# Two-level block product b of the output projection: earlier loads of w_out, its sums and y's on different engines, another order of splits

## The chip, the cores and the metric

The kernel runs on one core of a Trainium2 chip. The metric is the device time of one execution in microseconds, from the first to the last instruction of the core with what the launch adds around it. The kernel before took 803.74 us, the median of three runs (803.44 to 803.85).

## What is computed

One layer of a short-convolution mixer with a sandwich norm, on 1024 tokens of width 1024, with an inner width of 2048, all in float32:

```python
def short_conv_mixer(u, w_in, conv_w, w_out):
    z, bg, cg, v = jnp.split(u @ w_in.astype(u.dtype), 4, axis=-1)
    y = bg * causal_dwconv(cg * v, conv_w) * jax.nn.silu(z)
    return y @ w_out.astype(u.dtype)

# DEPTH is 1, so the layer is
u = rms_norm(x, pre_norm[0])
out = x + rms_norm(short_conv_mixer(u, sc_w_in[0], sc_conv_w[0], sc_w_out[0]), post_norm[0])
```

`u @ w_in` is 1024x1024 by 1024x8192, `y @ w_out` is 1024x2048 by 2048x1024.

## The kernel before

**Products.** Every matrix product is done as a 2x2 block product with seven block products instead of eight, called a, b, c, e, d, f, g. Products c, d, e, f and g take sums or differences of blocks as operands, a and b take plain blocks. Each operand is split into a high part (ScalarE rounds it to fp32r, L154) and a low part (VectorE subtracts the high part from the operand, L155), and each product is three matmuls: low times high, high times low, high times high.

**First stage.** The 2048 inner channels are 16 chunks of 128 columns. A chunk is two pairs: the even pair holds the columns of cg and v, the odd one those of z and bg; END = 31 is the last pair. From chunk 3 on the two pairs' products b are done together with a second level of the same scheme, seven small products a' to g' with 256 moving columns. The list `slots` is the order in which TensorE takes the products: for pair 31 it is a(31), e', g(30), c(31), f', e(31), d', d(31), f(31), g', g(31). After every slot the loop at L852 emits by hand what the other engines do then: weights' sums on GpSimd (`add_s`), splits (`prepare`), the convolution (L578 on ScalarE, L581 on VectorE), gates. Every engine works off its own instructions strictly in this written order. The finished chunk of y (`cv`) goes to DRAM (`y_d`, L243); `add_y` (L254) forms the sums of y that the last stage's products need and stores them in `s_d`; `add_t` does the same for w_out in `t_d`.

**Last stage.** y is the stationary side and w_out the moving side. Every block product but b is two halves h of four pages of 128x512; a half is `out_mm` on four PSUM banks, 48 matmuls of 512 columns. A half's operands come from `load_unit` (four loads of 256 KB each on SP's queue), and `split_unit` splits them into a buffer of the pool `up`, which has seven such buffers for both stages. Pages come from one pool of 36; a load or a sum that takes a page waits until the page's last reader is done.

**Product b of the last stage** has a second level of its own, `product_b` (L1052): seven small products `small_mm` of 24 matmuls with 256 columns, in the order a', b', e', c', d', f', g'. Its operands:

- `bu[0]`, `bu[1]`: the two groups of four pages of w_out; `by[0]`, `by[1]`: the same for y.
- `out_t` (L745) makes w_out's sums, four GpSimd instructions of 128x256 for each of four k: L754 changes the second half of `bu[0]` in place, L755 and L756 fill the pages `bu["cd"]`, L758 fills `bu["x"]`.
- `out_s` (L760) makes y's sums: kind "d" (L765) changes the second half of `by[0]` in place, kind "s" (L774 to L776) fills `by["ec"]` and `by["x"]`, which need `by[1]`.
- `out_split` splits them: A1 is `by[0]` after "d", A2 is `by[1]`, A3 is `by["ec"]`; B1 is `bu[0]` after L754, B2 is `bu[1]` as loaded, B3 is `bu["cd"]`; X is both "x". a' reads A1 and B1, b' reads A2 and B2, e' A3 and B1, c' A3 and B3, d' A1 and B3, f' X and B2, g' A2 and X. In the profile these are the tiles oA_b, oB_b and ox_b, the loaded pages ru_b and ry_b, the sums t_b and s_b, and the small products' banks pb_x, pb_y, pb_v.
- after each small product `small_add` (VectorE, L1050) adds its bank to `acc`. a', c', d' and g' share the bank pb_x, so c' must wait for the add of a', d' for that of c', g' for that of d'. Between these adds VectorE's order holds other splits: after the add of b' the four of X, after that of e' the four of the next unit (ou_c), and only then the add of c'.

`combine("a", q)` (L1003, ScalarE) copies the result of product a from PSUM to `acc`; `acc` lies where `cv` lay, so these copies also wait for the last `add_y`. B3's rounding stands behind them on ScalarE.

Of the kernel before, what the change touches and what calls it, by code (L numbers as in the profile page):

```python
# [21 lines left out]
def kernel(  # L22
# [16 lines left out]
    nc = tc.nc  # L39
# [5 lines left out]
    NC = CI // P  # L45
# [25 lines left out]
    def page(name, dtype=F32, shape=(HB,)):  # L71

        return pages.tile([P, *shape], dtype, tag="pg", name=name, bufs=PAGES)
# [79 lines left out]
    def split(src, hi, lo):  # L153
        nc.scalar.copy(hi, src)  # L154
        nc.vector.tensor_sub(lo, src, hi.bitcast(F32))  # L155
# [98 lines left out]
    def add_y(c):  # L254

        if c < CH:
            cv = done.pop(c)
            t = page(f"s3_{c}")
            nc.vector.tensor_sub(t, cv[:, :HB], cv[:, HB:])
            nc.sync.dma_start(s_d[:, SK["d"], c], t)  # L260
        else:
            cv, (t0, t1) = done.pop(c), far_y.pop(c)
            t2 = page(f"s4_{c}")
            nc.vector.tensor_add(t1, t1, cv[:, HB:])
            nc.vector.tensor_sub(t0, t1, t0)
            nc.vector.tensor_sub(t2, cv[:, :HB], t0)
            for k, t in zip("cef", (t0, t1, t2)):
                nc.sync.dma_start(s_d[:, SK[k], c - CH], t)
# [435 lines left out]
    CQ = CH // 2  # L704
    fetched, OP = [], {}

    def load_unit(side, i, h):
        js = slice(h * CQ, (h + 1) * CQ)
        far = slice(CH + h * CQ, CH + (h + 1) * CQ)
        if side == "u":  # L710
            plain_u = {"a": wov[:, js, :HB], "b": wov[:, far, :HB], "f": wov[:, far, HB:]}
            src = plain_u[i] if i in plain_u else t_d[:, TK[i], js]
        else:
            plain_y = {"a": y_d[:, js, :HB], "b": y_d[:, far, :HB], "g": y_d[:, far, HB:]}
            src = plain_y[i] if i in plain_y else s_d[:, SK[i], js]
        r = [page(f"r{side}_{i}{h}{k}") for k in range(CQ)]
        for k in range(CQ):
            nc.sync.dma_start(r[k], src[:, k])
        return r

    def fetch_unit():
        n = len(fetched)
        if n < len(UNITS):
            fetched.append(load_unit(*UNITS[n]))
# [8 lines left out]
    def split_pages(src, name):  # L733
        t = up.tile([P, 2, CQ, HB], F32R, tag="u", name=f"o{name}")
        for k in range(CQ):
            split(src[k], t[:, 0, k], t[:, 1, k])
        return t
# [4 lines left out]
    bu, by = {}, {}  # L742
    FB, SB = slice(0, HH), slice(HH, HB)

    def out_t(ks):  # L745

        for k in ks:
            b0, b1 = bu[0][k], bu[1][k]
            if k == 0:
                bu["cd"] = []  # L750
                bu["x"] = [page(f"t4_b{j}") for j in range(CQ // 2)]
            t = page(f"t23_b{k}")
            bu["cd"].append(t)
            nc.gpsimd.tensor_sub(b0[:, SB], b0[:, SB], b0[:, FB])  # L754
            nc.gpsimd.tensor_sub(t[:, FB], b1[:, SB], b0[:, SB])  # L755
            nc.gpsimd.tensor_sub(t[:, SB], t[:, FB], b0[:, FB])  # L756
            x = bu["x"][k // 2][:, k % 2 * HH : (k % 2 + 1) * HH]
            nc.gpsimd.tensor_sub(x, b1[:, FB], t[:, FB])  # L758

    def out_s(ks, kinds):  # L760

        for k in ks:
            a0, a1 = by[0][k], by[1][k]
            if kinds == "d":
                nc.gpsimd.tensor_sub(a0[:, SB], a0[:, FB], a0[:, SB])  # L765
                continue
            if k == 0:
                by["ec"] = []
                by["x"] = [page(f"s4_b{j}") for j in range(CQ // 2)]
            t = page(f"s12_b{k}")  # L770
            by["ec"].append(t)
            x = by["x"][k // 2][:, k % 2 * HH : (k % 2 + 1) * HH]

            nc.gpsimd.tensor_sub(t[:, SB], a1[:, SB], a0[:, SB])  # L774
            nc.gpsimd.tensor_add(t[:, FB], t[:, SB], a0[:, FB])
            nc.gpsimd.tensor_sub(x, a1[:, FB], t[:, SB])  # L776


    OUT_A = {"a'": ("A1", 0), "d'": ("A1", HH), "b'": ("A2", 0), "g'": ("A2", HH), "e'": ("A3", 0), "c'": ("A3", HH)}
# [3 lines left out]
    def out_split(n):  # L783
        if n == "X":
            t = up.tile([P, 2, 2, CQ, HH], F32R, tag="u", name="ox_b")
            for z, src in enumerate((by["x"], bu["x"])):
                for j in range(CQ // 2):
                    split(flat2(src[j]), t[:, z, 0, 2 * j : 2 * j + 2], t[:, z, 1, 2 * j : 2 * j + 2])
            ob_w[n] = t
        else:  # L790
            src = {"A1": (by, 0), "A2": (by, 1), "A3": (by, "ec"), "B1": (bu, 0), "B2": (bu, 1), "B3": (bu, "cd")}[n]
            ob_w[n] = split_pages(src[0][src[1]], f"{n}_b")

    def flat2(t):
        return t.rearrange("p (a b) -> p a b", b=HH)

    END = len(PAIRS) - 1
    TODO = {p: j for j, p in enumerate([8, 10, 12, 13, 14, 15, 16, 17])}

    def odd_t(p, steps):  # L800
        if p % 2 and p in TODO:
            add_t(TODO[p], steps)
# [32 lines left out]
    at, t = [], 0.0  # L835
# [16 lines left out]
    for n, (i, p) in enumerate(slots):  # L852
        if i[1:]:
            deep_product(p, i)
            prepare(n)
            deep_after(p, i)
            if i == "f'":
                odd_t(2 * p + 1, [0, 1])
            elif i == "g'":
                nc.scalar.activation(sn[2 * p + 1, "a"], sn[2 * p + 1, "a"], AF.Silu)  # L860
                odd_t(2 * p + 1, [3])
            continue
        product(p, i)
        prepare(n)
        after(p, i)
        q, prev = p + 1, p // 2 - 1
        if p == 2:
            first_chunk(i)
        if i == "c":
            if p % 2 and p // 2 < DEEP:  # L870
                nc.scalar.activation(sn[p, "a"], sn[p, "a"], AF.Silu)
            if p % 2 == 0 and p in TODO:
                fetch_t(TODO[p])
            if p % 2 == 0 and p > 2:
                fetch_s(prev)
            if p % 2 == 0 and p // 2 >= DEEP:
                deep_sums(p // 2, 1)
        elif i == "e":
            add_s(q, "ec")
        elif i == "d":  # L880
            if p + 2 <= END:
                fetch(p + 2)
            add_s(q, "d")
            if p in TODO and p % 2 == 0:
                add_t(TODO[p])
            if p % 2 == 0 and p > 2:
                add_y(prev)
        elif i == "f":
            add_s(q, "f")
            if p == 2:  # L890
                add_y(0)
        elif i == "g":
            if p % 2 and q <= END and q // 2 >= DEEP:
                deep_sums(q // 2, 0)
        elif i == "a":
            if p % 2 and p in TODO:
                fetch_t(TODO[p])
        if DEEP < NC and (i, p) in UNDER:
            UNDER[i, p]()
        if p == END - 1 and i in "cd":  # L900
            fetch_unit()
        if p == END:
            if i in "acdg":
                split_unit()
            if i in "ac":
                fetch_unit()
            if i in "ce":
                bu["ce".index(i)] = load_unit("u", "b", "ce".index(i))
            if i == "d":
                by[0] = load_unit("y", "b", 0)  # L910
                out_t([0, 1])
            elif i == "f":
                fetch_s(NC - 1)
                out_t([2, 3])
            elif i == "g":
                by[1] = load_unit("y", "b", 1)
                out_s(range(CQ), "d")
                out_s(range(CQ), "s")
    mixed.close()
    p2 = ctx.enter_context(tc.tile_pool(name="p2", bufs=1, reuse_waits="tile"))  # L920

# [96 lines left out]
    def finish_row(t):  # L1018
        finish(t)
        if t + 2 < NT:  # L1020
            load_res(t + 2)
# [40 lines left out]
                for q in (0, 1) if i == "f'" else (2, 3):  # L1062
                    early_half(q)

    for i in ("A1", "B1"):
        out_split(i)
    add_y(NC - 1)
    out_split("A2")
    for n, (i, h) in enumerate(OUT[:-2]):
        if i == "b":  # L1070
            if h == 0:
                product_b()
            continue
        if (i, h) == ("f", 0):
            load_res(0)
            load_res(1)
        for q in range(TH):
            out_mm(i, h, q)
        if i == "a":
            if h == 0:  # L1080
                out_split("B2")
                out_split("A3")
                fetch_unit()
        else:
            for _ in "uy":
                split_unit()
                fetch_unit()
        if h == 1:
            for q in range(TH):
                combine(i, q)  # L1090
                if i == "f" and q > 0:
                    finish_row(q - 1)
            if i == "a":
                out_split("B3")
# [31 lines left out]
```

## Time and profile before

| | |
|---|---|
| time, median of 3 runs | 803.74 us (803.44 to 803.85) |
| the profiled execution: its time | 806.15 us |
| its span, first to last instruction | 804.3 us |
| TensorE busy | 783.3 us, 97% of the span |
| VectorE busy | 620.2 us, 77% |
| GpSimd busy | 393.8 us, 49% |
| ScalarE busy | 341.2 us, 42% |
| mean granted TensorE clock | 0.99 |

How to read it: times of an engine's rows count from the span's start. A busy TensorE is not one at its peak, since matmuls are pipelined and overlap in the records; the distance between starts tells the rate. "idle before <- releaser" names what the engine had last waited for. Lines of the kernel are written L155; a helper's line stands for all its uses, so groups are told apart by the tiles that they write and read.

### The profile page before, as it was taken

How to read it: one execution, taken by the hardware profiler on the slowest of the kernel's cores; microseconds unless marked ns; L12 is line 12 of the kernel's file. 1: busy time of each engine (PE TensorE's matmuls, PEld its weight loads, DVE VectorE, ACT ScalarE, POOL GpSimd, SP SyncE). 2: the span in 40 equal slices, each digit the busy share in tenths (PEclk: the TensorE clock that was granted, in tenths of full speed). 3: DMA queues.
4: the chain of work that ended last, by engine and by line, in shares of the span. 5: the costliest groups of instructions: out<-in, count | busy, mean ns of one | idle time of the engine just before them, and what ended most of it. 6: DMA issues, size and time to landing. Idle time of an engine off the chain costs nothing.

```text
span 804.3 us, 11017 instructions
## 1 busy us (share of the span) xinstructions
PE 783.3 (97%) x3800; PEld 661.3 (82%) x3800; DVE 620.2 (77%) x847; ACT 341.2 (42%) x622; POOL 393.8 (49%) x289
## 2 busy tenths in 40 slices
PE   9999999999999999999999999999999968999995
PEld 8888888888888888888888888888888858888884
DVE  6899667978777888888686867768688698844665
ACT  7555425343424342434433343434345174655431
POOL 2616579646647373748483746556471970000020
PEclk9999999999999999999999999999999988999999
DMA  9111330407162565654150606152339469753047
GB/s 335 34 53 37 109 117 28 138 21 236 47 202 84 203 187 199 199 177 157 53 172 26 196 2 195 39 158 78 119 106 318 159 220 376 254 187 108 1 126 241
DMA packets 108329, 114.53 MB, mean 142 GB/s; under 512 B 6585, under 2 KB 72177, under 8 KB 108273
## 3 DMA queue, kind: packets, MB, share of 16 engines
q1 hardware_dynamic: 108256, 113.82, 43.1%
q8 instruction: 30, 0.49, 0.3%
q14 instruction: 27, 0.21, 0.1%
q10 hardware_dynamic: 16, 0.00, 0.0%
HBM read 84.44 MB, written 29.36 MB: 141 GB/s over the span
## 4 chain that ended last, share of the span: by engine, by line
PE 87%; DMA 4%; DVE 3%; POOL 2%; ACT 1%; issue 1%; POOLq 0%; DVEq 0%; SPq 0%; ACTq 0%
PE px L189 14%; PE px L188 14%; PE px L190 14%; PE pv L188 7%; PE pv L189 7%; PE pv L190 7%; DMA xr<-in_x 2%; PE po_x L946 2%; PE po_x L948 2%; PE po_x L947 2%; PE po_v L948 2%; PE po_v L946 2%; PE po_v L947 2%; PE px L687 1%; PE px L686 1%; PE px L685 1%
## 5 line engine op out<-in xcount | busy, mean ns | idle before, releaser
L217 POOL TENSOR_TENSOR sne<-sne,cv 128x512 f32<-128x512 f32 x15 | 25.1, 1672 | 161.4 <-DVE sne L215 161.4
L988 POOL TENSOR_TENSOR acc<-acc,xr 128x512 f32<-128x512 f32 x4 | 6.5, 1624 | 121.1 <-DVE acc L987 117.9
L581 DVE SCALAR_TENSOR_TENSOR cv<-gpad,cw,cv 128x1024 f32<-128x1024 f32 x32 | 42.0, 1313 | 17.3 <-ACT cv L578 16.7
L155 DVE TENSOR_TENSOR wel<-se,weh 128x512 fp32r<-128x512 f32 x31 | 52.1, 1682 | 3.2 <-ACT weh L154 3.2
L146 POOL TENSOR_TENSOR se<-raw,raw 128x512 f32<-128x512 f32 x31 | 52.2, 1684 | 3.0 <-PE px L190 2.5
L150 POOL TENSOR_TENSOR sf<-raw,sc 128x512 f32<-128x512 f32 x31 | 53.0, 1710 | 0.0
L148 POOL TENSOR_TENSOR sc<-se,raw 128x512 f32<-128x512 f32 x31 | 50.1, 1617 | 2.4
L196 ACT COPY snc<-px 128x512 f32<-128x512 f32 x31 | 18.2, 586 | 73.3 <-PE px L190 73.3
L225 POOL TENSOR_TENSOR gpad<-snc,sne 128x512 f32<-128x512 f32 x15 | 20.1, 1339 | 59.3 <-DVE snc L220 59.3
L188 PE MATMUL pv<-u_e,wel 128*128 128x512 f32 x124 | 48.6, 392 | 0.0
L188 PE MATMUL px<-u_g,wgl 128*128 128x512 f32 x124 | 48.5, 391 | 0.0
L189 PE MATMUL px<-u_d,wdh 128*128 128x512 f32 x124 | 48.6, 392 | 0.0
L189 PE MATMUL pv<-u_e,weh 128*128 128x512 f32 x124 | 48.6, 392 | 0.0
L189 PE MATMUL px<-u_a,wah 128*128 128x512 f32 x124 | 48.6, 392 | 0.0
L188 PE MATMUL px<-u_a,wal 128*128 128x512 f32 x124 | 48.6, 392 | 0.0
L196 ACT COPY sna<-px 128x512 f32<-128x512 f32 x30 | 17.5, 583 | 73.2 <-PE px L190 48.7
L188 PE MATMUL px<-u_d,wdl 128*128 128x512 f32 x124 | 48.5, 391 | 0.0
L189 PE MATMUL px<-u_g,wgh 128*128 128x512 f32 x124 | 48.4, 391 | 0.0
L188 PE MATMUL pv<-u_f,wfl 128*128 128x512 f32 x124 | 48.3, 390 | 0.0
L188 PE MATMUL px<-u_c,wcl 128*128 128x512 f32 x124 | 48.2, 389 | 0.0
L190 PE MATMUL px<-u_a,wah 128*128 128x512 f32 x124 | 48.2, 389 | 0.0
L190 PE MATMUL px<-u_c,wch 128*128 128x512 f32 x124 | 48.2, 389 | 0.0
(409 smaller groups left out, 2610.2 us busy)
## 6 DMA issues: line engine op xcount, KB each, us to landing
raw<-in_sc_w_in SPq DMA_DIRECT2D x128, 256.0 KB, 4.2
y_d<-cv SPq DMA_DIRECT2D x16, 512.0 KB, 3.0
s_d<-s SPq DMA_DIRECT2D x32, 256.0 KB, 2.3
t<-in_sc_w_out SPq DMA_DIRECT2D x32, 256.0 KB, 4.2
t_d<-t SPq DMA_DIRECT2D x32, 256.0 KB, 2.6
s<-y_d SPq DMA_DIRECT2D x16, 256.0 KB, 4.2
xr<-in_x SPq DMA_DIRECT2D x16, 256.0 KB, 4.9
xa<-in_x SPq DMA_DIRECT2D x4, 512.0 KB, 5.1
```

Source lines behind the costliest of these rows:

```text
L146: nc.gpsimd.tensor_add(t, block(p, 1, 0), block(p, 1, 1))
L148: nc.gpsimd.tensor_sub(t, sums[p, "e"], block(p, 0, 0))
L150: nc.gpsimd.tensor_sub(t, block(p, 0, 1), sums[p, "c"])
L155: nc.vector.tensor_sub(lo, src, hi.bitcast(F32))
L188: nc.tensor.matmul(ps, lo, UH[i][:, k], start=first and k == 0, stop=False, skip_group_check=True)
L189: nc.tensor.matmul(ps, hi, UL[i][:, k], start=False, stop=False, skip_group_check=True)
L190: nc.tensor.matmul(ps, hi, UH[i][:, k], start=False, stop=last, skip_group_check=True)
L196: nc.scalar.copy(t, banks[p, "v" if i == "e" else "x"])
L581: nc.vector.scalar_tensor_tensor(cv, gpad[:, j : j + L], tap(c, j), cv, op0=ALU.mult, op1=ALU.add)
L946: nc.tensor.matmul(ps, lo, u[:, 0, k], start=first, stop=False, skip_group_check=True)
L947: nc.tensor.matmul(ps, hi, u[:, 1, k], start=False, stop=False, skip_group_check=True)
L948: nc.tensor.matmul(ps, hi, u[:, 0, k], start=False, stop=last, skip_group_check=True)
```

## The change

Three things move, and no computation is added or left out:

- y's sums for product b, `out_s`, go from GpSimd to VectorE, four instructions of kind "d" and twelve of kind "s".
- The eight loads of w_out's blocks (`bu`) move from slots c and e of pair 31 to slots d and f of pair 30, and so ahead of the second units' loads of product a on SP's queue; w_out's sums (`out_t`) move from d and f of pair 31 to c and e of pair 31. On GpSimd they now stand ahead of the last pair's gates (L217, L223) instead of around them.
- The order of splits. Before: A1, B1, `add_y`, A2, then B2 and A3. After, in VectorE's order: B2, B1, the four "d", A1, the twelve "s", A2, A3, `add_y`, with B3 behind as before.

```diff
@@ out_s @@
             if kinds == "d":
-                nc.gpsimd.tensor_sub(a0[:, SB], a0[:, FB], a0[:, SB])
+                nc.vector.tensor_sub(a0[:, SB], a0[:, FB], a0[:, SB])
                 continue
...
-            nc.gpsimd.tensor_sub(t[:, SB], a1[:, SB], a0[:, SB])
-            nc.gpsimd.tensor_add(t[:, FB], t[:, SB], a0[:, FB])
-            nc.gpsimd.tensor_sub(x, a1[:, FB], t[:, SB])
+            nc.vector.tensor_sub(t[:, SB], a1[:, SB], a0[:, SB])
+            nc.vector.tensor_add(t[:, FB], t[:, SB], a0[:, FB])
+            nc.vector.tensor_sub(x, a1[:, FB], t[:, SB])
@@ the loop over slots @@
+        if p == END - 1 and i in "df":
+            bu["df".index(i)] = load_unit("u", "b", "df".index(i))
         if p == END:
             if i in "acdg":
                 split_unit()
             if i in "ac":
                 fetch_unit()
             if i in "ce":
-                bu["ce".index(i)] = load_unit("u", "b", "ce".index(i))
+                out_t(([0, 1], [2, 3])["ce".index(i)])
             if i == "d":
                 by[0] = load_unit("y", "b", 0)
-                out_t([0, 1])
             elif i == "f":
                 fetch_s(NC - 1)
-                out_t([2, 3])
             elif i == "g":
                 by[1] = load_unit("y", "b", 1)
+                out_split("B2")
+                out_split("B1")
                 out_s(range(CQ), "d")
-                out_s(range(CQ), "s")
+                out_split("A1")
@@ ahead of the last stage's products @@
-    for i in ("A1", "B1"):
-        out_split(i)
-    add_y(NC - 1)
-    out_split("A2")
@@ after product a's first half @@
             if h == 0:
-                out_split("B2")
+                out_s(range(CQ), "s")
+                out_split("A2")
                 out_split("A3")
+                add_y(NC - 1)
                 fetch_unit()
```

## The prediction

> **What bounds the kernel now.** The page first: TensorE is busy for nearly the whole span.
>
> ```profile
> span 804.3 us, 11017 instructions
> PE 783.3 (97%) x3800; PEld 661.3 (82%) x3800; DVE 620.2 (77%) x847; ACT 341.2 (42%) x622; POOL 393.8 (49%) x289
> ```
>
> So only what TensorE waits for, or does slowly, can be won. Its waits over the whole span, longest first:
>
> ```profile
> PE pb_x L1043 <- DVE acc L1050: 3.6, 1, 3.6
> PE pb_y L1044 <- DVE oB_b L155: 2.8, 1, 2.8
> PE pb_y L1043 <- DVE oA_b L155: 2.7, 1, 2.7
> ```
>
> All three lie in product b of the last stage, and all end on VectorE. Busy time by stretch (after the stretch: its length, then PE, PEld, DVE, ACT, POOL; the granted clock is behind the engines):
>
> ```profile
> 660.00:670.00 10.00, 8.53 (x57) 8.35 (x58) 9.90 (x18) 6.44 (x14) 0.00 (x0) 0.77 1.02 355
> 670.00:680.00 10.00, 6.38 (x37) 6.18 (x36) 7.83 (x14) 3.18 (x6) 0.00 (x0) 0.74 1.05 400
> 700.00:710.00 10.00, 10.00 (x46) 8.29 (x45) 1.27 (x3) 3.08 (x7) 0.00 (x0) 1.00 0.37 129
> 780.00:790.00 10.00, 10.00 (x46) 8.29 (x45) 7.87 (x21) 1.61 (x6) 3.03 (x2) 1.00 0.84 254
> ```
>
> Product b also runs at a lower clock (0.77, 0.74), while from 700 on TensorE is full at clock 1.00: a gain in product b reaches the end whole. TensorE's order of time there:
>
> ```profile
> 627.44 0.39 PE L946 MATMUL po_x<-ou_a,oy_a 128*128 128x512 f32 x1
> 649.20 0.28 PE L1043 MATMUL pb_x<-oB_b,oA_b 128*128 128x256 f32 x1
> 658.07 0.55 PE L1043 MATMUL pb_y<-oB_b,oA_b 128*128 128x256 f32 x1 [2.72 <-DVE oA_b L155]
> 675.48 0.58 PE L1043 MATMUL pb_x<-oB_b,oA_b 128*128 128x256 f32 x1 [3.62 <-DVE acc L1050]
> 675.86 0.41 PE L1044 MATMUL pb_x<-oB_b,oA_b 128*128 128x256 f32 x1
> 676.08 0.41 PE L1045 MATMUL pb_x<-oB_b,oA_b 128*128 128x256 f32 x1
> 686.81 0.28 PE L1045 MATMUL pb_x<-ox_b,oA_b 128*128 128x256 f32 x1
> 686.93 0.40 PE L946 MATMUL po_x<-ou_c,oy_c 128*128 128x512 f32 x1
> ```
>
> Product b takes 37.7 us (649.20 to 686.93). Its 168 matmuls at the late spacing of 0.12 (686.81 to 686.93) would need 20.2. After a gap they start 0.21 apart (675.86 to 676.08). The start at 675.48 is d', which waited for VectorE's add of c'.
>
> VectorE's order of time up to that add:
>
> ```profile
> 630.92 0.72 DVE L230 TENSOR_TENSOR cv<-cv,sna 128x512 f32<-128x512 f32 x1 [0.29 <-ACT sna L860]
> 631.56 5.21 DVE L155 TENSOR_TENSOR oy_a<-ry_a,oy_a 128x512 fp32r<-128x512 f32 x4
> 644.10 4.71 DVE L155 TENSOR_TENSOR oA_b<-ry_b,oA_b 128x512 fp32r<-128x512 f32 x4 [7.33 <-ACT oA_b L154]
> 648.73 4.65 DVE L155 TENSOR_TENSOR oB_b<-ru_b,oB_b 128x512 fp32r<-128x512 f32 x4
> 653.30 1.22 DVE L264 TENSOR_TENSOR s<-s,cv 128x512 f32<-128x512 f32 x1
> 656.72 4.07 DVE L155 TENSOR_TENSOR oA_b<-ry_b,oA_b 128x512 fp32r<-128x512 f32 x4
> 660.71 2.49 DVE L155 TENSOR_TENSOR oB_b<-ru_b,oB_b 128x512 fp32r<-128x512 f32 x4
> 672.33 2.49 DVE L155 TENSOR_TENSOR ou_c<-ru_c,ou_c 128x512 fp32r<-128x512 f32 x4
> 674.74 0.69 DVE L1050 TENSOR_TENSOR acc<-pb_x,acc 128x512 f32<-128x512 f32 x1
> ```
>
> VectorE idles 7.33 us until A1's operand exists, and is then busy to the add. Four splits take 4.6 from start to start while GpSimd works beside them (644.10 to 648.73) and 2.41 when it does not (672.33 to 674.74): GpSimd's sums slow the splits as well as keep them waiting.
>
> **The change part by part: VectorE from L230's end to the add of c'.** Before, 631.64 to 675.43, 43.8 us. Removed: the idle time, 7.33; what GpSimd's work beside it cost, the sums of y being gone from it: oy_a 2.0 (5.21 to an estimated 3.2, as the gate L223 still runs beside a part), A1 2.2, B1 2.2 (4.57 to 2.41), add_y 1.2 (653.30 to 656.72 is 3.4; three at the 0.72 of L230 are 2.2), A2 1.6 (3.99 to 2.41). Together 16.5.
>
> Added: four sums "d" and twelve "s". VectorE's nearest instruction of that size, both operands in SBUF, is dw:
>
> ```profile
> 618.11 0.42 DVE L155 TENSOR_TENSOR dw<-raw,dw 128x256 fp32r<-128x256 f32 x1
> 618.44 0.69 DVE L155 TENSOR_TENSOR wgl<-raw,wgh 128x512 fp32r<-128x512 f32 x1
> ```
>
> It holds the queue for 0.33; one that needs its predecessor's result would take the full 0.42 and a little, 0.45. "d": 1.3. "s": between 4.0 and 5.4, I take 4.5, as only one of the three depends on the instruction just ahead.
>
> Then a new wait. add_y now stands after A3, and ScalarE's copies of product a wait for it, with B3's roundings queued behind them and VectorE's B3 splits behind these; TensorE's c' waits for them through the add of a':
>
> ```profile
> 659.07 2.04 ACT L1003 COPY acc<-po_x 128x512 f32<-128x512 f32 x4
> 660.98 2.21 ACT L154 CAST oB_b<-t_b 128x512 fp32r<-128x512 f32 x4
> ```
>
> VectorE idles for the copies and the first rounding, 2.04 and about 0.6: 2.7. Added together: 8.5. Net: 8.0 us shorter.
>
> **w_out's sums in GpSimd's idle time.** The cover is real, but not free:
>
> ```profile
> 607.34 1.81 SPq L718 DMA_DIRECT2D ru_a<-in_sc_w_out  x4
> DMA to landing us min/median/max: 5.3/5.6/5.6
> 624.64 1.61 POOL L217 TENSOR_TENSOR sne<-sne,cv 128x512 f32<-128x512 f32 x1 [15.71 <-DVE sne L215]
> L754 POOL TENSOR_TENSOR ru_b<-ru_b x4: 732/958/1201, 626.2 to 639.7; 128x256 f32<-128x256 f32 x4
> ```
>
> The eight loads take the place on SP's queue where ru_a's stood, 607.34, and land in 5.3 to 5.6 (ru_b's own row): the first group from 612.9, the second, queued behind it, from about 615.6. GpSimd sits idle 15.71 until 624.64. Sixteen sums at the median 0.96 are 15.3, so all but the first run from about 615.6 to 630. ru_a and ry_a of the second units come some 5 us later, by about 622, well ahead of their roundings (ry_a's precede the splits at 631.56). What the sums now run beside is VectorE's path to g(31):
>
> ```profile
> 615.36 2.50 DVE L155 TENSOR_TENSOR oy_a<-ry_a,oy_a 128x512 fp32r<-128x512 f32 x4 [1.93 <-ACT oy_a L154]
> 619.38 0.69 DVE L236 TENSOR_TENSOR gpad<-px,sna 128x512 f32<-128x512 f32 x1
> 621.29 2.60 DVE L581 SCALAR_TENSOR_TENSOR cv<-gpad,cw,cv 128x1024 f32<-128x1024 f32 x2 [1.23 <-ACT cv L578]
> 623.81 0.68 DVE L215 TENSOR_TENSOR sne<-px,sne 128x512 f32<-128x512 f32 x1
> 624.41 4.68 DVE L155 TENSOR_TENSOR ou_a<-ru_a,ou_a 128x512 fp32r<-128x512 f32 x4
> 624.55 0.50 PE L188 MATMUL px<-u_g,wgl 128*128 128x512 f32 x1
> ```
>
> VectorE ran this stretch with GpSimd idle, and without slack: L215 ends at 624.49 and g(31) starts at 624.55. With GpSimd beside them four splits cost 4.68 (ou_a) instead of 2.50: 2.0 more here, as the sums begin a little after 615.36; dw and wgl at the same ratio 0.8 more. L581 has no row beside a 128x256 sum: nothing to 2.3 (the splits' ratio on 2.60); I take 0.5, since it has a third, per-channel operand and another form than the splits. L215 and g(31) come 3.3 late: a new stall of TensorE.
>
> After L215 the splits ou_a still have GpSimd beside them, for a little less long (0.3), so L230 ends 3.0 late (bounds: nothing, if the sums do not collide, to 5.0 with L581 at its upper bound).
>
> **The sum.** 3.0 - 8.0 = -5.0: the add of c' ends at 670.4, d' starts at 670.5 instead of 675.48. TensorE is there earlier: product a starts at 630.7, takes its 21.8 (627.44 to 649.20), b starts at 652.5; a', b' and e' need 8.6; c' has to wait for the add of a', which ends 6.7 ahead of that of c' (X, ou_c, three adds), at 663.7, and ends by 666.7. So the stall ahead of g(31) is absorbed, even with some 3 us of slow matmuls behind it; what decides is VectorE's queue. The gap ahead of d' is 3.8, above 2.72 and 3.62, so d', f' and g' take their 11.45 again (675.48 to 686.93). The profiled execution took 806.15 at a span of 804.3; less 5.0 it is 801.15. The runs' median of 803.74 lies 2.41 below the profiled one: **798.7**.
>
> **Rivals.** (1) No collision: the second group of blocks lands late, or the splits are not slowed, and L215 stays where it was. Then the gain is the whole 8.0: 795.7. For it: the landing time is an estimate, and a late landing moves the sums beyond 620. Against: GpSimd would then sit beside ou_a as before, and L581 follows.
>
> (2) The clock holds. c' waits some 2.7 us itself; if it runs at 0.21, it takes 5.1 and ends at 668.9, and d' follows after 1.6 only. If the clock then counts TensorE as busy, the 72 matmuls of d', f' and g' need 8.6 instead of 11.45: 2.8 less, 795.9. Against: after the gap of 2.72 matmuls were slow (0.55 for the first), and after 3.62 they stayed so for 6 us. TensorE: Matmul & The Clock Gate of the Trainium skill ("What's actually happening") puts the drop at an idle window of about 3.4 us that runs free of the kernel; by it a gap of 3.8 need not hold a whole window. The row of 2.72 speaks for an earlier drop.
>
> (3) VectorE becomes the bound by its new sums, and the kernel is slower. If a sum costs VectorE what it cost GpSimd, up to 1.2 (L754's maximum), sixteen cost 19.2 instead of 5.8: 13.4 more, 812.1. It turns slower above 0.67 each (5.0 spread over sixteen, on 0.36). For it: they are in place or feed each other. Against: 0.42 for dw, and GpSimd idle by then.
>
> (4) L581 is slowed like the splits: 2.3 in place of 0.5, g(31) and L230 come 1.8 later still, 800.5. For it: it reads two tensors from SBUF as the splits do. Against: another form. The GPSIMD Engine Reference of the Trainium skill ("Specifications") speaks for it: GpSimd shares its SBUF interfaces with VectorE, and they contend where a VectorE instruction has two SBUF inputs. No row here shows L581 beside such sums.
>
> (5) The idle time is too short for w_out's sums: at 1.2 each they end near 634, L217 and L223 follow to 637, `cv` is as late as before (636.2), and by[1] lands at about 645, when VectorE wants it for the twelve sums at 646. Another 3 us late costs 2: about 801.
>
> **How the numbers follow.** Forecast 0.38, rival (1) 0.20, (2) 0.13, (3) 0.07, (4) 0.14, (5) 0.08. Within 0.2% (1.6 us) is about what a measurement cannot tell from no change. Slower: (3) and a little of (5), 0.08. The same: most of what is left of (5), 0.05. Faster: the forecast, (1), (2), (4) and the rest of (5), 0.87. The forecast's own range is 796.5 to 801 (twelve sums 4.0 to 5.4, L581 nothing to 2.3, a smaller collision). The range of 8 in 10 takes in (1), (2), (4) and most of (5), and leaves out (3): 793.5, a little above (1) with (2), to 802.
>
> **What would show it.** Right: VectorE's 128x256 sums at 0.33 to 0.45 each; no 7 us idle on VectorE after oy_a; splits four in 2.4 from A1 on; a gap of TensorE before g(31) of 2 to 4 us; the largest wait of TensorE still d' for L1050, near 3.8, at about 670; ScalarE's copies of product a released by add_y. Wrong: g(31) on time, or a wait of TensorE for A2, A3 or a load, or the last stage's c not starting 4 to 6 us earlier than 686.93.

## The result, and the profile after

The kernel after takes 800.1 us, the median of six runs (799.36 to 801.16), beside 803.64 (803.44 to 803.93) for the kernel before on the same chip: a ratio of 0.9957, 95% interval 0.9944 to 0.9970, a gain of 3.5 us. Two later runs of the kernel before took 1311 us at a granted clock of 0.56, and no ratio counts them. The profiled execution took 800.7 us at a span of 798.7. The head of its page:

```profile
span 798.7 us, 11006 instructions
PE 781.9 (98%) x3800; PEld 660.5 (83%) x3800; DVE 617.3 (77%) x863; ACT 341.1 (43%) x622; POOL 378.4 (47%) x273
```

TensorE's waits of the kernel after, longest first (engine, tile, line, releaser: us in total, times, longest). Those for A2 and B2 are gone, that of d' is as long as it was, and a new one stands ahead of g(31):

```profile
PE pb_x L1045 <- DVE acc L1052: 3.9, 2, 3.6
PE px L188 <- DVE sne L215: 2.7, 1, 2.7
```

TensorE's order of time in the kernel after (start, duration, in brackets what it had waited for):

```profile
627.46 0.79 PE L188 MATMUL px<-u_g,wgl 128*128 128x512 f32 x1 [2.67 <-DVE sne L215]
632.75 0.63 PE L948 MATMUL po_x<-ou_a,oy_a 128*128 128x512 f32 x1
...
654.91 0.28 PE L1045 MATMUL pb_x<-oB_b,oA_b 128*128 128x256 f32 x1
...
663.99 0.36 PE L1045 MATMUL pb_x<-oB_b,oA_b 128*128 128x256 f32 x1 [0.29 <-DVE acc L1052]
...
670.70 0.38 PE L1045 MATMUL pb_x<-oB_b,oA_b 128*128 128x256 f32 x1 [3.61 <-DVE acc L1052]
...
680.93 0.40 PE L948 MATMUL po_x<-ou_c,oy_c 128*128 128x512 f32 x1
```

g(31) starts 2.91 late, and TensorE runs slowly until product a starts at 632.75. Product b starts at 654.91 instead of 649.20, but has no gap above 0.3 us until d', which starts at 670.70 instead of 675.48. The last stage's c starts at 680.93 instead of 686.93.

VectorE's order of time in the kernel after:

```profile
615.64 3.59 DVE L155 TENSOR_TENSOR oy_a<-ry_a,oy_a 128x512 fp32r<-128x512 f32 x4 [1.43 <-ACT oy_a L154]
...
620.03 1.22 DVE L155 TENSOR_TENSOR wgl<-raw,wgh 128x512 fp32r<-128x512 f32 x1
...
621.51 0.67 DVE L236 TENSOR_TENSOR gpad<-px,sna 128x512 f32<-128x512 f32 x1
623.41 3.40 DVE L581 SCALAR_TENSOR_TENSOR cv<-gpad,cw,cv 128x1024 f32<-128x1024 f32 x2 [1.23 <-ACT cv L578]
626.73 0.68 DVE L215 TENSOR_TENSOR sne<-px,sne 128x512 f32<-128x512 f32 x1
...
634.44 3.58 DVE L155 TENSOR_TENSOR oy_a<-ry_a,oy_a 128x512 fp32r<-128x512 f32 x4
637.95 4.89 DVE L155 TENSOR_TENSOR oB_b<-ru_b,oB_b 128x512 fp32r<-128x512 f32 x8
642.76 1.42 DVE L765 TENSOR_TENSOR ry_b<-ry_b 128x256 f32<-128x256 f32 x4
...
646.52 0.41 DVE L774 TENSOR_TENSOR s_b<-ry_b,ry_b 128x256 f32<-128x256 f32 x1
646.96 0.42 DVE L775 TENSOR_TENSOR s_b<-s_b,ry_b 128x256 f32<-128x256 f32 x1
...
651.02 2.49 DVE L155 TENSOR_TENSOR oA_b<-ry_b,oA_b 128x512 fp32r<-128x512 f32 x4
...
660.74 2.50 DVE L155 TENSOR_TENSOR oB_b<-t_b,oB_b 128x512 fp32r<-128x512 f32 x4 [2.76 <-ACT oB_b L154]
...
669.97 0.68 DVE L1052 TENSOR_TENSOR acc<-pb_x,acc 128x512 f32<-128x512 f32 x1
```

Eight splits (B2 and B1) now take 4.8, the four "d" 1.35 from start to start, the twelve "s" 4.50 (646.52 to 651.02). The only idle time left ahead of the add of c' is the 2.76 before B3, behind ScalarE's copies, which wait for `add_y` (ScalarE's row of the kernel after):

```profile
658.14 2.05 ACT L1005 COPY acc<-po_x 128x512 f32<-128x512 f32 x4 [6.72 <-DVE s L266]
```

GpSimd's order of time in the kernel after, with w_out's sums ahead of the gate L217; the two that start beside L581 take 1.58 and 1.59, where the sixteen of before took 0.73 to 1.20:

```profile
613.98 0.82 POOL L754 TENSOR_TENSOR ru_b<-ru_b 128x256 f32<-128x256 f32 x1 [5.22 <-DMA ru_b<-in_sc_w_out]
616.59 0.95 POOL L755 TENSOR_TENSOR t_b<-ru_b,ru_b 128x256 f32<-128x256 f32 x1 [1.79 <-DMA ru_b<-in_sc_w_out]
...
624.14 1.58 POOL L755 TENSOR_TENSOR t_b<-ru_b,ru_b 128x256 f32<-128x256 f32 x1
...
632.67 1.29 POOL L217 TENSOR_TENSOR sne<-sne,cv 128x512 f32<-128x512 f32 x1
```

So the profiled executions differ by 4.78 us at d', 6.00 at c and 5.6 in span, but the medians by 3.5 only. One place to look for the rest is the very end. First the kernel before, then the kernel after, TensorE's last matmul and VectorE's wait for the last residual:

```profile
795.53 0.39 PE L948 MATMUL po_x<-ou_g,oy_g 128*128 128x512 f32 x1
...
799.82 0.75 DVE L993 SCALAR_TENSOR_TENSOR gx<-gx,rs_post,xr 128x512 f32<-128x512 f32 x1 [1.42 <-DMA xr<-in_x]
```

```profile
789.53 0.39 PE L950 MATMUL po_x<-ou_g,oy_g 128*128 128x512 f32 x1
...
794.14 0.75 DVE L995 SCALAR_TENSOR_TENSOR gx<-gx,rs_post,xr 128x512 f32<-128x512 f32 x1 [1.80 <-DMA xr<-in_x]
```

From the last matmul's start to the end of the span it is 8.77 before (804.3 less 795.53) and 9.17 after: the end waits for a transfer, and for how long differs. On SP's queue the last residual's load stands behind the stores of an earlier row (kernel after):

```profile
788.33 0.49 SPq L965 DMA_DIRECT2D out<-c  x1
788.91 0.90 SPq L962 DMA_DIRECT2D xr<-in_x  x2
```

### The profile page after: what moved, and what is told of

Its sections match the earlier page's. It is cut to its first block, busy times and chain, and to the rows that moved or that the text cites. A ratio compares the mean times of both kernels' runs of the same rounds, so it can differ in the third digit from the quotient of the medians.

```text
span 798.7 us, 11006 instructions
## 1 busy us (share of the span) xinstructions
PE 781.9 (98%) x3800; PEld 660.5 (83%) x3800; DVE 617.3 (77%) x863; ACT 341.1 (43%) x622; POOL 378.4 (47%) x273
## 4 chain that ended last, share of the span: by engine, by line
PE 90%; DMA 5%; DVE 2%; ACT 2%; issue 0%; SPq 0%; POOLq 0%; DVEq 0%; ACTq 0%
PE px L188 14%; PE px L189 14%; PE px L190 14%; PE pv L188 7%; PE pv L189 7%; PE pv L190 7%; PE po_x L948 3%; PE po_x L949 3%; PE po_x L950 3%; DMA xr<-in_x 2%; PE po_v L949 2%; PE po_v L948 2%; PE po_v L950 2%; PE px L687 1%; PE px L686 1%; PE px L685 1%
## 5 line engine op out<-in xcount | busy, mean ns | idle before, releaser
L217 POOL TENSOR_TENSOR sne<-sne,cv 128x512 f32<-128x512 f32 x15 | 24.8, 1650 | 145.6 <-DVE sne L215 145.6
L581 DVE SCALAR_TENSOR_TENSOR cv<-gpad,cw,cv 128x1024 f32<-128x1024 f32 x32 | 43.0, 1343 | 17.3 <-ACT cv L578 16.7
L189 PE MATMUL px<-u_g,wgh 128*128 128x512 f32 x124 | 49.4, 398 | 0.0
L190 PE MATMUL px<-u_g,wgh 128*128 128x512 f32 x124 | 49.2, 397 | 0.0
L190 PE MATMUL pv<-u_f,wfh 128*128 128x512 f32 x124 | 48.3, 389 | 0.0
```

Source lines behind the costliest of these rows:

```text
L189: nc.tensor.matmul(ps, hi, UL[i][:, k], start=False, stop=False, skip_group_check=True)
L190: nc.tensor.matmul(ps, hi, UH[i][:, k], start=False, stop=last, skip_group_check=True)
L217: nc.gpsimd.tensor_mul(t, t, cvs[c][:, HB:])
L581: nc.vector.scalar_tensor_tensor(cv, gpad[:, j : j + L], tap(c, j), cv, op0=ALU.mult, op1=ALU.add)
```

## The experiments

Each ratio is to the kernel before, run on the same chip, with its 95% interval. "d'" and "c" are the starts in that kernel's profile; "end" is the span less the start of the last matmul.

| kernel | median us | ratio | d' | c | end |
|---|---|---|---|---|---|
| before, again | 803.74 | 1.0001 (0.9987 to 1.0015) | 675.49 | 685.65 | 7.55 |
| after, again | 800.31 | 0.9957 (0.9944 to 0.9971) | 670.46 | 681.47 | 8.92 |
| 1 before, y's sums on VectorE | 799.91 | 0.9954 (0.9937 to 0.9970) | 670.94 | 681.17 | 8.03 |
| 2 after, y's sums on GpSimd | 802.18 | 0.9976 (0.9964 to 0.9988) | 673.40 | 682.14 | 8.67 |
| 3 after, w_out's sums late | 803.17 | 0.9985 (0.9971 to 0.9999) | 673.80 | 682.53 | 10.17 |
| 4 after, add_y early | 797.84 | 0.9916 (0.9901 to 0.9931) | 668.20 | 679.29 | 7.41 |
| 5 after, add of c' first | 797.56 | 0.9920 (0.9907 to 0.9933) | 668.51 | 677.24 | 9.66 |
| 6 after, 4 and 5 | 793.85 | 0.9875 (0.9856 to 0.9894) | 665.73 | 674.47 | 8.13 |
| 7 before, residual early | 803.35 | 0.9990 (0.9979 to 1.0000) | 676.02 | 686.25 | 7.14 |
| 8 after, residual early | 798.56 | 0.9927 (0.9910 to 0.9944) | 670.90 | 680.95 | 7.15 |
| 9 after, 4, 5 and residual early | 792.02 | 0.9847 (0.9831 to 0.9863) | 665.39 | 674.13 | 7.07 |
| 10 before, 1, 5 and residual early | 795.54 | 0.9890 (0.9874 to 0.9907) | 669.57 | 678.31 | 7.09 |

**Both kernels once more, unchanged.** The kernel before:

> The kernel before, unchanged, profiled once more. Theory: the 2.41 us by which its profiled execution lay above the runs' median belong to that execution alone, a longer wait or a longer stretch of slow clock in product b; then this execution takes 803.4 to 804.5, and TensorE's last-stage c starts at about 684.5 to 685.5 instead of 686.93. Rival: profiling itself costs the kernel before 2.4 us; then it takes about 806 again and c starts near 686.9. In the kernel after the profiled execution lay only 0.6 above the median.

Measured: 803.55 us at a span of 801.8, 2.5 less than the first profile. Rows of this second profile of before:

```profile
675.49 0.58 PE L1043 MATMUL pb_x<-oB_b,oA_b 128*128 128x256 f32 x1 [3.61 <-DVE acc L1050]
...
685.65 0.40 PE L946 MATMUL po_x<-ou_c,oy_c 128*128 128x512 f32 x1
...
797.24 0.75 DVE L993 SCALAR_TENSOR_TENSOR gx<-gx,rs_post,xr 128x512 f32<-128x512 f32 x1 [0.45 <-DMA xr<-in_x]
```

d' stands where it stood, to 0.01 us. From there to c it is 10.16 instead of 11.45: 1.29 less slow clock. The end is 1.22 shorter. Together 2.51, the whole difference. Theory right, but only half of it lay in product b, so c came at 685.65, later than 685.5. The kernel after:

> The kernel after, unchanged, profiled once more. Theory (VectorE's order is the same to 0.1 us in every execution, and executions differ only in how long TensorE stays at a lower clock after a gap): L1052's add of c' starts within 0.2 us of where it stands in the first profile, counted from product b's own operands (A1's splits), TensorE's three waits have the same lengths to 0.2 us, and the time differs from 800.1 by no more than 2.5. Rival: VectorE's order shifts against itself by over 0.5 us.

From A1's splits to the add of c' it is 25.86 in the first profile (644.11 to 669.97) and 25.87 in the second (643.85 to 669.72). The wait ahead of d' is 3.61 again; that ahead of g(31) is 3.26 instead of 2.67 and that ahead of c' 0.95 instead of 0.29, both more than the 0.2 that the theory allowed. Ahead of g(31) the splits oy_a, beside w_out's sums, took 4.17 instead of 3.59: what the sums cost there differs by half a us between executions.

**1: the engine move alone**

```diff
@@ out_s, in the kernel before @@
-                nc.gpsimd.tensor_sub(a0[:, SB], a0[:, FB], a0[:, SB])
+                nc.vector.tensor_sub(a0[:, SB], a0[:, FB], a0[:, SB])
...
-            nc.gpsimd.tensor_sub(x, a1[:, FB], t[:, SB])
+            nc.vector.tensor_sub(x, a1[:, FB], t[:, SB])
```

> The kernel before, with y's sums on VectorE and nothing else changed, so that they stand ahead of the splits A1 and B1 in its order. Theory: the twelve sums wait for by[1]'s loads until 645 to 647 and hold all splits behind them, so product b starts 3 to 5 us late (652 to 654), but the splits behind then run alone, four in 2.41; the add of c' comes within 3 us of where it was (675.43) and the time is 801 to 806. Rival: the engine move alone gives most of the change's gain, 799 to 801.

The rival was right: 799.91, the change's whole gain. The theory had by[1] land at 645 to 647; it lands by 641. VectorE's order of time in this kernel:

```profile
636.64 3.60 DVE L765 TENSOR_TENSOR ry_b<-ry_b 128x256 f32<-128x256 f32 x4
...
640.84 0.43 DVE L774 TENSOR_TENSOR s_b<-ry_b,ry_b 128x256 f32<-128x256 f32 x1 [0.60 <-DMA ry_b<-y_d]
...
670.20 0.69 DVE L1050 TENSOR_TENSOR acc<-pb_x,acc 128x512 f32<-128x512 f32 x1
```

The add of c' starts at 670.20, in the kernel after at 669.97. Here w_out's sums on GpSimd still slow "d" (3.60 for 1.42) and some of "s"; in the kernel after they do not, but VectorE starts this part 2.9 late and waits 2.76 behind `add_y`. The two bills are about equal.

**2: everything but the engine move**

```diff
@@ out_s, in the kernel after @@
-                nc.vector.tensor_sub(a0[:, SB], a0[:, FB], a0[:, SB])
+                nc.gpsimd.tensor_sub(a0[:, SB], a0[:, FB], a0[:, SB])
...
-            nc.vector.tensor_sub(x, a1[:, FB], t[:, SB])
+            nc.gpsimd.tensor_sub(x, a1[:, FB], t[:, SB])
```

> The kernel after, with y's sums (four d, twelve s) on GpSimd again, everything else as after. Theory (the engine of these sums is what the change lives on: on GpSimd they take about 1 us each, are started late and double the splits beside them): sums of 0.9 to 1.2 us on GpSimd, splits four in 4.6 beside them, VectorE waiting several us for oA_b ahead of A3's splits, d' at 674 to 678 and 804 to 808 us. Rival (only the earlier sums of w_out and the order of splits matter): 799 to 801.

802.18, between the theory's 804 and the rival's 801: neither was right. With everything else as after, the engine move is worth some 1.5 us (0.9976 to 0.9957). Groups of GpSimd and VectorE's B2 and B1 in this kernel:

```profile
L774 POOL TENSOR_TENSOR s_b<-ry_b,ry_b 128x256 f32<-128x256 f32 x4 | 4.8, 1188 | 0.0
```

```profile
639.07 9.26 DVE L155 TENSOR_TENSOR oB_b<-ru_b,oB_b 128x512 fp32r<-128x512 f32 x8
```

The sums cost 1.19 each and nearly double the time of the splits beside them (9.26 for 4.89), as expected, but A3's splits did not wait: d' comes at 673.40, 2.7 after that of the kernel after.

**3: w_out's sums in their old slots, the loads early**

```diff
@@ the loop over slots, in the kernel after @@
-            if i in "ce":
-                out_t(([0, 1], [2, 3])["ce".index(i)])
+            if i in "df":
+                out_t(([0, 1], [2, 3])["df".index(i)])
```

> The kernel after, with w_out's sums emitted in the slots of before (d and f of pair 31), the loads staying early. Theory (the sums delay VectorE's path to g(31)): L581 takes 2.60 instead of 3.40, L215 ends near 624.5 instead of 627.4, and g(31) starts within 0.3 of that without a slow stretch. The sums then lie beside oy_a, B2 and B1 instead, with about the same cost per split (2.4 more per four), so d' comes within 1 us of 670.7 and the time stays at 799.5 to 801. Rival (the collision ahead of g(31) costs the end its 3 us): d' at about 667.7 and 797 us. Second rival (L581 is late for another reason): L215 stays at 626.7.

The place of the collision was as the theory said, its price was not. VectorE in this kernel:

```profile
621.27 2.61 DVE L581 SCALAR_TENSOR_TENSOR cv<-gpad,cw,cv 128x1024 f32<-128x1024 f32 x2 [1.22 <-ACT cv L578]
623.80 0.68 DVE L215 TENSOR_TENSOR sne<-px,sne 128x512 f32<-128x512 f32 x1
...
631.54 5.23 DVE L155 TENSOR_TENSOR oy_a<-ry_a,oy_a 128x512 fp32r<-128x512 f32 x4
636.70 9.23 DVE L155 TENSOR_TENSOR oB_b<-ru_b,oB_b 128x512 fp32r<-128x512 f32 x8
```

L581 is back at 2.61 and L215 on time. But oy_a and eight splits run beside the sums: 1.7 and 4.3 dearer, 6.0, against the 2.9 saved ahead of g(31). d' is 3.1 later than in the kernel after, the ratio 0.9985 instead of 0.9957, 2.3 us. So the collision is not avoided by the change, but moved to where it costs VectorE half (2.9 for 6.0), and within the new order of splits the early sums are worth some 2.3 us.

**4: `add_y` ahead of the twelve sums**

```diff
@@ after product a's first half, in the kernel after @@
+                add_y(NC - 1)
                 out_s(range(CQ), "s")
                 out_split("A2")
                 out_split("A3")
-                add_y(NC - 1)
```

> The kernel after, with add_y of the last chunk ahead of the twelve sums instead of behind A3. Theory (add_y behind A3 holds ScalarE's copies of product a, B3's roundings behind them, and so VectorE's B3 splits): VectorE's 2.76 us idle ahead of B3 falls below 0.3, d' starts at 668.0 to 668.4 instead of 670.70, and the time falls by 2 to 2.7 to about 797.7. Rival: the copies wait for product a's end at about 654.9 anyhow or A2 and A3 come too late (TensorE waits over 1 us for oA_b ahead of b' or e'), and the time stays at 799.5 to 800.7.

As the theory said: 797.84 us. ScalarE and VectorE in this kernel:

```profile
653.74 2.04 ACT L1005 COPY acc<-po_x 128x512 f32<-128x512 f32 x4
```

```profile
658.25 2.49 DVE L155 TENSOR_TENSOR oB_b<-t_b,oB_b 128x512 fp32r<-128x512 f32 x4
```

Neither waits any more, and d' starts at 668.20, 2.5 earlier.

**5: the add of c' ahead of four splits**

```diff
@@ product_b, in the kernel after @@
-            elif i in ("e'", "c'", "d'", "f'"):
-                split_unit()
-                fetch_unit()
+            elif i in ("c'", "d'", "f'"):
+                for _ in "uy" if i == "c'" else "u":
+                    split_unit()
+                    fetch_unit()
```

> The kernel after, with the four splits that stand between the add of e' and the add of c' put behind the add of c'. Theory (d' waits for VectorE's order, not for work that it needs): the add of c' ends within 0.8 of c's end, about 667.2, and d' starts at 667.3 to 667.8 instead of 670.70, its gap shrinking from 3.61 to under 1; without a long gap TensorE keeps its full clock and d', f', g' take 8.6 to 9.2 instead of 10.2. c of the last stage starts 3 to 4.5 earlier, 676.4 to 678, and the time is 795.8 to 797.2. Rival: the splits put off come back as a wait of g' for the add of d' or of c for its operands, over 2 us, and the time stays above 799.

VectorE's add of c' and TensorE's d' in this kernel:

```profile
667.77 0.68 DVE L1052 TENSOR_TENSOR acc<-pb_x,acc 128x512 f32<-128x512 f32 x1
```

```profile
668.51 0.38 PE L1045 MATMUL pb_x<-oB_b,oA_b 128*128 128x256 f32 x1 [1.20 <-DVE acc L1052]
```

The gap ahead of d' fell from 3.61 to 1.20 (expected under 1; the add of c' starts at 667.77, right behind that of e'), d' comes 0.7 later than the 667.8 expected at most, and from d' to c it is 8.73 (668.51 to 677.24), full rate. 797.56 is a little above the expected 797.2, with an end of 9.66.

**6: both**

> The kernel after, with both edits: add_y of the last chunk ahead of the twelve sums, and the add of c' ahead of the four splits. Theory (both waits were VectorE's order and lie one behind the other): VectorE goes from A3's splits to B3's without a wait, the add of a' comes 2.5 us earlier than with the second edit alone (663.37), c' has no wait for it over 0.5, and d' waits less than 1.5; c of the last stage starts 1.5 to 3 us earlier than with the second edit alone, and the time is 794.5 to 796.5. Rival: TensorE is then the bound (product b starts at 652 to 655 and needs 20.2 us) and little is won over one edit alone: 796.8 to 797.8.

The two add up: 793.85, below the range. TensorE's waits in this kernel:

```profile
PE px L188 <- DVE sne L215: 2.7, 1, 2.7
PE pb_x L1045 <- DVE acc L1052: 1.5, 2, 1.2
```

**7 to 10: the residual four rows ahead**

```diff
@@ ahead of product f @@
-            load_res(0)
-            load_res(1)
+            for t in range(4):
+                load_res(t)
@@ finish_row @@
-        if t + 2 < NT:
-            load_res(t + 2)
+        if t + 4 < NT:
+            load_res(t + 4)
```

On the kernel before:

> The kernel before, with the residual's pages loaded four rows ahead instead of two. Theory (part of what the profiled execution of before lay above the others, 8.77 us from the last matmul's start to the end against 7.55, is VectorE's wait for the last residual, 1.42 us, 0.45 there): that wait goes, the end comes 7.1 us after the last matmul's start in every execution, and the time falls by 0.5 to 1.5 to 802.5 to 803.5. Rival: the residual lands late because of the transfers around it, not because of its place behind the stores, and wait and time stay.

On the kernel after:

> The kernel after, with the same edit of the residual's loads. In its two profiles the end came 9.17 and 8.92 us after the last matmul's start, with a wait of 1.80 and 1.34. Theory: the end eats 1 to 2 us of what product b gained; without the wait it comes after 7.1, the time is 798.0 to 799.2, and the distance to the same edit of before is 4 to 5 us. Rival: the distance stays at the 3.6 of the unedited kernels.

On 6:

> The kernel after, with add_y ahead of the twelve sums, the add of c' ahead of the four splits, and the residual loaded four rows ahead. Theory: the end comes 7.1 us after the last matmul's start instead of 8.13, so 792.5 to 793.3 against 793.85. Rival: no gain, 793.5 to 794.2.

And on 1 with the edit of 5:

> The kernel before, with three edits: y's sums on VectorE, the add of c' ahead of the four splits, the residual four rows ahead; w_out's loads, its sums and the order of the first splits stay as before. Theory (moving w_out's work pays only once the wait behind add_y is gone, then by some 3 us, since VectorE's B1 and A1 come earlier and product b runs without a gap): add of c' at 667.8, c of the last stage at 677.5 to 679, 795.5 to 797. Rival (w_out's place is worth nothing here either): c at 674.5 as with the other edits, 792.5 to 793.5.

The end came after 7.07 to 7.15 in all four, as expected, with no wait for xr left. The last rows in the kernel after with this edit:

```profile
789.55 0.39 PE L950 MATMUL po_x<-ou_g,oy_g 128*128 128x512 f32 x1
...
792.12 0.75 DVE L995 SCALAR_TENSOR_TENSOR gx<-gx,rs_post,xr 128x512 f32<-128x512 f32 x1
```

Before and after, 7 and 8, are now 4.79 apart (803.35 to 798.56), about as far as their d' (4.78 in the first profiles, 5.12 in these). By the two ratios and their intervals the distance lies between some 3.5 and 6.7, so it is not clear of the 3.5 of the unedited kernels. 9 came out half a us better than expected, 792.02. In 10 the add of c' starts at 668.83 instead of 667.8, as c' itself ends later (0.56 of waiting for it); time and c are as the theory said. 10 against 9 prices w_out's early place and the new order of splits together, with both waits gone: 795.54 to 792.02, 3.5 us. In the change as it was made (1 against the kernel after) the two together are worth nothing, although within the new order the early sums alone are worth 2.3 us (3). No run has w_out's early place with the old order of splits.

## Why the prediction was right, and where it was off

**The sum for VectorE held.** From oy_a's start to the add of c' it was 43.18 (631.56 to 674.74) and is 35.53 (634.44 to 669.97): 7.65 shorter, forecast 8.0. The idle 7.33 is gone; "d" cost 1.35 for 1.3, "s" 4.50 for 4.5, the new wait 2.76 for 2.7. oy_a gave back 1.6 instead of 2.0. That the new wait is ScalarE's copies behind `add_y` is shown by 4.

**The collision ahead of g(31) held as a whole.** L215 came 2.92 late (623.81 to 626.73), forecast 3.3. Its parts were mis-sized against each other: oy_a 1.1 dearer instead of 2.0, as the second group's sums start only at 616.59; dw and wgl 0.7 instead of 0.8; L581 0.8 instead of 0.5; and oy_a started 0.3 later, which the sum did not have. That these errors partly cancel is luck.

**d' followed VectorE**: forecast 670.5, measured 670.70, after a gap of 3.61 for 3.8. TensorE's late start and slow matmuls were absorbed, but only just: product b started at 654.91 instead of the 652.5 forecast, and c' waited 0.29 for the add of a' instead of some 2.7.

**The clock after d'** stayed low for a shorter time than "11.45 again": 10.23, and 11.01 in the second profile. Rival (2) came half true in the first. It is no property of the change: the kernel before shows 11.45 and 10.16.

**The step that was off** is the last: "The runs' median of 803.74 lies 2.41 below the profiled one: 798.7", with "a gain in product b reaches the end whole" behind it. Up to there the sum gave 801.15 for the profiled execution, and 800.7 was measured. That these are so close is partly luck: the stretch from d' to c took 1.22 less than forecast, and the end 0.40 more than before. But the 2.41 were nothing that every profiled execution carries: 1.29 of slow clock and 1.22 of waiting for residuals (the second profile of before). Another run of before reached 806.98. The profiled execution of after lies 0.6 above its median. Against the second profile of before the kernel after, profiled again, gains 4.2 at c and 2.8 in span, since its end is 8.92 to 7.55. With the residual early in both the distance is 4.79, with ratios of 0.9990 and 0.9927. By the ratios that edit gains 0.9 us on before and 2.4 on after: this fits a longer end of the kernel after, but lies within the intervals of the ratios. Whether its end is longer by rule stays open: it was 9.17 and 8.92 in two profiles, 8.77 and 7.55 before, and 7.41 to 10.17 in the experiments with the residual as it was.

**The other rivals.** No collision (1): refuted by L215's 2.92. VectorE's sums dear (3): 0.34 to 0.45 each. L581 slowed like the splits (4): 3.40, where 4.9 would have been needed. Idle time too short (5): the sums end at 632.7, y_d is issued at 635.70 and not later than before (636.24), and VectorE waits for no load.

## What to carry to other kernels

Ask what an engine's next instruction really needs: here two waits of some 2.5 us were only the written order, ahead of B3 and ahead of the add of c', and turning them round gave 6.5 us (800.31 to 793.85), more than the change. In the change w_out's early place and the new order of splits earned nothing on top of the engine move: that order had put a new wait behind `add_y`. When one profiled execution lies off the median, find which rows differ in a second profile before subtracting the difference from a forecast. A gain in mid-kernel must also be followed through the last rows: a load queued behind stores can take part of it back.

## What the runs showed of the hardware

**Equal gaps, unequal clocks.** Ahead of g(31) TensorE waited 2.67 us in four executions. Its 12 matmuls then took 2.85 (experiment 6), 2.87 (experiment 8), 4.45 (experiment 5) and 5.29 (the kernel after). Busy time from 628 to 630, first in experiment 8, then in the kernel after, with a granted clock (the third number from the end) of 1.00 and 0.50:

```profile
628.00:630.00 2.00, 2.00 (x10) 1.63 (x9) 2.00 (x3) 0.00 (x0) 1.92 (x3) 1.00 0.00 0
```

```profile
628.00:630.00 2.00, 2.00 (x6) 1.56 (x5) 2.00 (x3) 0.00 (x0) 1.92 (x3) 0.50 0.00 0
```

Rows of experiment 8, TensorE:

```profile
627.60 0.50 PE L188 MATMUL px<-u_g,wgl 128*128 128x512 f32 x1 [2.67 <-DVE sne L215]
...
630.47 0.39 PE L948 MATMUL po_x<-ou_a,oy_a 128*128 128x512 f32 x1
```

After 2.27 (experiments 4 and 9) they took 2.85 both times, after 3.23 (experiment 2) and 3.26 (after, again) 4.40 and 4.45. After a d' gap of 3.61 or 3.62 the clock was low in all five profiles that have one: the stretch from d' to c took 1.4 to 2.7 us more than the 8.73 to 8.74 of experiments 5 and 6, whose gap was 1.20. TensorE: Matmul & The Clock Gate of the Trainium skill ("What's actually happening") says that the window that decides runs free of the kernel; the four outcomes of one gap fit that. It also asks for an idle window of some 3.4 us, and here 2.67 was enough twice.

**GpSimd beside VectorE.** Splits with two operands in SBUF took up to 1.9 times as long beside sums of 128x256 (9.26 to 4.89), L581, which also reads two tensors there, 1.3 times (3.40 to 2.60), and L236, which reads one from PSUM, did not change (0.67 to 0.69). SBUF — State Buffer of the Trainium skill ("Who interferes with whom") says that a VectorE instruction with at most one input in SBUF, outside the modes that use two ports, does not contend with GpSimd, and L236 agrees.
